# A streaming encoder layer on one core: the first adaLN columns shared between two engines, and second norm and token forms as one chain

## The chip, the core and the metric

The kernel runs on one core of a Trainium2 chip. The core has a matrix engine (TensorE, PE in the profile), two element-wise engines (VectorE, DVE; ScalarE, ACT), a general engine (GpSimd, POOL), and SyncE (SP), whose queue issues most transfers. Each works through its own list of instructions in order and waits at semaphores for the others. TensorE reads SBUF and writes PSUM, which is a set of banks that other engines must empty. The metric is the device time of one execution in microseconds, lower is better.

## The reference, cut to what matters

One layer over 1024 prompt frames and 32 sample frames, width 1024, in float32. The two groups of frames have a conditioning vector each, so that every adaLN column exists twice.

```python
mod = jax.nn.silu(c) @ w_ada + b_ada                       # (D,) @ (D, 6 D)
sh1, sc1, gt1, sh2, sc2, gt2 = jnp.split(mod[:, None, :], 6, axis=-1)
h = rmsnorm(x, g_mix) * (1 + sc1) + sh1
u = h @ w_in                                               # attention, mLSTM and gate columns
...                                                        # band attention, mLSTM
merged = (jax.nn.sigmoid(ga) * (ya @ w_br_att) + jax.nn.sigmoid(gm) * (ym @ w_br_mlstm))
x = x + gt1 * (merged @ w_out)
h2 = rmsnorm(x, g_ffn) * (1 + sc2) + sh2
g, up = jnp.split(h2 @ w_gate_up, 2, axis=-1)
x = x + gt2 * ((jax.nn.silu(g) * up) @ w_down)
```

Keys and values of the last 512 frames are outputs too. A final RMSNorm ends it.

## The kernel before, in words

All activations lie transposed, features on the 128 partitions in 8 row tiles of 1056 tokens (1024 + 32), which are cut into three column tiles of 352 (`TILES`). A float32 product is made of three fast ones (`PASSES`): each operand is split into a rounded part, which ScalarE writes, and the rest, which an element-wise engine subtracts. The helper `unit` computes one block of 128 output features on one column tile: 8 row tiles x 3 passes = 24 products into one PSUM bank (`mm`, three banks). `split_to` splits weights (L373 ScalarE, L374 VectorE or GpSimd).

The order on PE, ACT, DVE and POOL is the order in which the program is written; SP's order is a scheduler's. `Weights` loads and splits weight blocks ahead of their use: `advance` splits up to `ahead` blocks past the one in use and loads three raw blocks. `Side` runs generators beside the units: each unit gives 4 ticks, and a job takes `steps / ticks` steps a tick; `drain` runs what is left of it.

**Front.** While the inputs load, x is transposed (L300), its squares are summed, and `first_ada` multiplies silu(c) with the first 2048 columns of `w_ada`: for each of 8 row tiles k, 16 blocks of 128 columns on TensorE (L338), where the moving operand repeats the two conditions over 128 columns. Blocks 0 to 7 are the shift (bank psS), 8 to 15 the scale (psT). After the first k come the broadcast of the norm's factor (L263, L267), eight multiplications of x with it (L325) and the split of the first two weight blocks. `first_mod` adds the bias to the columns. `first_units` then runs the first two blocks of `w_in` (k and v of head pair 0) on all tiles at once, with `first_h` per row tile: VectorE scales and shifts (L362), ScalarE rounds (L363), VectorE subtracts (L364), and 18 products follow (L429). The third block (q) is an ordinary unit.

**Norm and FFN.** `second_norm(tiles)` is a side job: sums of squares by one-column products (L1478, L1479), a power on GpSimd (L1484), a `yield`, a broadcast through TensorE (L263), and then a step for each row tile: scale (L1495, VectorE), shift and round (L1496, ScalarE), low part (L1506, VectorE). It runs for the first column tile beside the last two column tiles of `w_out`, and for the other two beside the first FFN units. The first three FFN blocks are plain (`gate_unit`, `up_unit`, with the product on VectorE, L1643). Beside them `early_forms` makes sums and differences of the normed tokens (L1550, in turn on GpSimd and VectorE, L1560 and L1563 the split), four turns over row tiles. The later FFN blocks multiply these forms (`fifteen_products`, L1688), and `late_forms` makes the last of them. Before L1688 starts, the PSUM pools of the plain units are closed, so that their last evacuation must be done.

## Time and profile before

| | |
|---|---|
| median of 3 runs | 1672.52 us (1672.14 to 1672.92) |
| the profiled execution | 1671.17 us |
| its span, first to last instruction | 1669.2 us |
| mean granted TensorE clock | 0.99 |
| TensorE busy | 1605.7 us (96%) |
| VectorE, ScalarE, GpSimd busy | 67%, 47%, 32% |
| DMA | 192.47 MB, 115 GB/s on the mean |

In the rows, L and a number is a line of the kernel before. A timeline row is the start in us, the length, the engine, the line, the operation, output<-input, shapes, the count of merged instructions and, in brackets, the idle time before it and who ended it. A row of a line or tile has min/median/max of one instruction in ns, then first and last start. A matrix product is two rows of the profile for four-byte operands of the front (L338, L263, L1478), one for the rounded ones (L429, L407).

### The profile page before, as it was taken

The page shows a single profiled execution, that of the slowest core. Times are in us where ns is not written, and L with a number is a line of the kernel's source. Part 1 is how long each engine was busy: PE and PEld are TensorE (multiplying, and loading weights), DVE is VectorE, ACT ScalarE, POOL GpSimd, SP SyncE. Part 2 cuts the span into 40 slices and gives each one's busy share as a digit, 9 for nine tenths or more (in the row PEclk, how much of TensorE's full clock was granted, in tenths as well). Part 3 has the DMA queues.
Part 4 walks back from the last instruction along what each step waited for, and adds up shares of the span by engine and source line. Part 5 has one row for each costly group of instructions (what it writes and reads, how often), then busy time and mean ns, then how long its engine had stood idle before and what let it go on. Part 6 is the DMA issues. An engine that isn't in the chain of part 4 may idle for free.

```text
span 1669.2 us, 27636 instructions
## 1 busy us (share of the span) xinstructions
PE 1605.7 (96%) x10396; PEld 1580.4 (95%) x10396; DVE 1113.6 (67%) x2083; ACT 777.3 (47%) x1724; POOL 534.1 (32%) x540
## 2 busy tenths in 40 slices
PE   7989999999999999999999997999999999998997
PEld 6879999999999999999999997999999999998997
DVE  5446564646685755546655578989888886698754
ACT  3255454543455634444434444454544444444443
POOL 0043333423342311000012136556565652233101
PEclk9999999999999999999999899999999999999999
DMA  9533223332222332474453210222223136426453
GB/s 342 208 99 102 82 85 94 90 101 94 77 87 75 68 94 72 116 273 155 127 149 115 81 52 26 89 78 90 90 65 102 65 100 221 138 68 223 138 157 122
DMA packets 210328, 192.47 MB, mean 115 GB/s; under 512 B 10570, under 2 KB 180530, under 8 KB 209170
## 3 DMA queue, kind: packets, MB, share of 16 engines
q1 hardware_dynamic: 210194, 190.70, 36.3%
q8 instruction: 82, 1.34, 0.3%
q14 instruction: 52, 0.43, 0.1%
HBM read 152.19 MB, written 41.63 MB: 116 GB/s over the span
## 4 chain that ended last, share of the span: by engine, by line
PE 78%; DVE 8%; issue 3%; ACT 2%; POOL 1%; DMA 1%; DVEq 0%; POOLq 0%; ACTq 0%
PE mm L407 35%; PE psb L1688 23%; PE psb L2044 5%; PE mm L794 3%; PE psb L1929 3%; PE psV L694 2%; PE psS L636 1%; DVE wsp L374 1%; PE psT L663 1%; DVE s L1563 1%; DVE sl L1550 1%; DVE s L374 1%; POOL t L1253 1%; DMA wraw<-in_w_down_dram 1%; DVE s L1951 1%
## 5 line engine op out<-in xcount | busy, mean ns | idle before, releaser
L407 PE MATMUL mm<-s,wsp 128*128 128x352 f32 x4176 | 707.1, 325 | 10.4 <-DVE t L1643 4.5
L407 PEld LDWEIGHTS mm<-s,wsp 128*128 128x128 f32 x4176 | 671.6, 189 | 14.5 <-DVE t L1643 5.1
L1688 PE MATMUL psb<-s,wsp 128*128 128x352 f32 x2544 | 424.2, 324 | 16.2 <-DVE t L1643 6.1
L1688 PEld LDWEIGHTS psb<-s,wsp 128*128 128x128 f32 x2544 | 413.5, 190 | 18.9 <-issue 9.8
L374 DVE TENSOR_TENSOR wsp<-wraw,wsp 128x512 fp32r<-128x512 f32 (+1 forms) x284 | 246.4, 885 | 131.3 <-ACT wsp L373 129.7
L373 ACT ACTIVATE wsp<-wraw 128x512 fp32r<-128x512 f32 x342 | 202.4, 617 | 145.1 <-PE psb L1688 83.8
L656 POOL TENSOR_SCALAR st<-st,mx 128x640 f32<-128x640 f32 (+5 forms) x72 | 56.7, 787 | 192.7 <-DVE mx L655 178.4
L374 POOL TENSOR_TENSOR wsp<-wraw,wsp 128x512 fp32r<-128x512 f32 x58 | 76.6, 1342 | 108.3 <-ACT wsp L373 107.8
L1110 DVE SCALAR_TENSOR_TENSOR t<-wa,cmix,t 128x512 f32<-128x512 f32 x112 | 89.8, 807 | 8.6 <-DMA wa<-in_w_ada_dram 8.2
L2044 PE MATMUL psb<-s,wsp 128*128 128x352 f32 x528 | 86.9, 324 | 0.0
L2044 PEld LDWEIGHTS psb<-s,wsp 128*128 128x128 f32 x528 | 84.9, 188 | 0.0
L650 DVE CUSTOM_DVE_ANT_0 st<-psS,bias 128x640 f32<-128x640 f32 (+5 forms) x72 | 44.5, 618 | 57.0 <-PE psS L636 44.0
L1688 PE MATMUL psb<-x,wsp 128*128 128x352 f32 x432 | 79.3, 322 | 2.9 <-DVE x L1563 2.9
L651 ACT ACTIVATE st<-st,mx 128x640 f32<-128x640 f32 (+5 forms) x72 | 47.9, 665 | 68.9 <-DVE mx L650 68.8
L1525 POOL TENSOR_TENSOR t<-t,sl 128x352 f32<-128x352 f32 x18 | 17.6, 978 | 185.1 <-ACT sl L1523 185.1
L1688 PEld LDWEIGHTS psb<-x,wsp 128*128 128x128 f32 x432 | 71.0, 188 | 3.2 <-DVE x L1563 3.2
L670 ACT ACTIVATE pT<-psT 128x640 fp32r<-128x640 f32 (+3 forms) x80 | 38.6, 493 | 72.4 <-PE psT L663 57.3
L1726 DVE TENSOR_TENSOR t<-t,psb 128x352 f32<-128x352 f32 x120 | 60.4, 511 | 4.6 <-PE psb L1688 4.4
L1330 POOL TENSOR_TENSOR wraw<-wraw 128x512 f32<-128x512 f32 x25 | 37.0, 1480 | 78.3 <-DVE wsp L374 77.3
L675 DVE TENSOR_TENSOR pT<-psT,pT 128x640 fp32r<-128x640 f32 (+3 forms) x80 | 44.0, 558 | 20.6 <-ACT pT L670 20.4
L1330 POOL TENSOR_TENSOR wraw<-wraw,raw 128x512 f32<-128x512 f32 x33 | 55.8, 1703 | 0.9
L794 PE MATMUL mm<-s,s 128*128 128x264 f32 (+3 forms) x432 | 54.8, 283 | 0.0
(336 smaller groups left out, 2311.3 us busy)
## 6 DMA issues: line engine op xcount, KB each, us to landing
wraw<-in_w_in_dram SPq DMA_DIRECT2D x40, 512.0 KB
wraw<-in_w_gate_up_dram SPq DMA_DIRECT2D x33, 512.0 KB
wa<-in_w_ada_dram SPq DMA_DIRECT2D x64, 256.0 KB
wraw<-in_w_down_dram SPq DMA_DIRECT2D x32, 512.0 KB
a_d<-t SPq DMA_DIRECT2D x22, 528.0 KB
g_d<-t SPq DMA_DIRECT2D x16, 528.0 KB
x<-xres SPq DMA_DIRECT2D x16, 528.0 KB
t<-g_d SPq DMA_DIRECT2D x16, 528.0 KB
```

The lines of the kernel that those rows point to most:

```text
L373: act.activation(dst[:, 0], src, AF.Copy)
L374: eng.tensor_tensor(dst[:, 1], src, f(dst[:, 0]), op=ALU.subtract)
L407: pe.matmul(pt[:, :hi - lo], wt[(w0 + k) // 4][:, a, (w0 + k) % 4], xt[k][:, b, lo:hi], start=(k == 0 and q == 0), stop=(k == n - 1 and q ...
L651: act.activation(st[:n, :w], st[:n, :w], AF.Exp, bias=mx[:n, 1:2], scale=-1.0, accum_out=mx[:n, 2:3])
L656: pool.tensor_scalar(st[:n, :w], st[:n, :w], mx[:n, 3:4], 1.0, op0=ALU.mult, op1=ALU.mult)
L794: pe.matmul(pt[:n, :wd], hs[k][:, a, i * P:i * P + n], whl[b][:, k, :wd], start=(k == 0 and q == 0), stop=(k == KD - 1 and q == 2))
L1110: dve.scalar_tensor_tensor(ac[:, c], wa, cmix[:, c, k:k + 1], ac[:, c], op0=ALU.mult, op1=ALU.add)
L1330: pool.tensor_tensor(a(dst), a(x), a(y), op=op)
L1688: pe.matmul(acc, wt[:, a, k], x[k][:, b], start=(start and not onto and k == 0 and q == 0), stop=(stop and k == 3 and q == 2), skip_group_ ...
L1726: dve.tensor_tensor(c, c, y, op=ALU.add if sign > 0 else ALU.subtract)
L1929: pe.matmul(acc, wt[k // 4][:, u, k % 4], piece_of[k, i][:, v], start=(k == 0 and q == 0), stop=(k == KP - 1 and q == 2))
L2044: pe.matmul(acc, wt[(k - k0) // 4][:, u, (k - k0) % 4], piece_of[k, 2][:, v], start=(k == 0 and q == 0), stop=(k == NF - 1 and q == 2))
```

## The change

- *adaLN columns.* TensorE keeps blocks 6 to 15. For blocks 0 to 5 VectorE accumulates, for each condition, the row tiles of `w_ada` times silu(c) in SBUF (`acv`, 128 x 768, 16 passes), and 12 one-column products (6 blocks x 2 conditions) sum over the partitions. Two of the eight row tiles' loads and the weight loads change places in the program; the split of the first two weight blocks moves from k = 0 to k = 3, and a third raw block is asked for before `xres` is written.
- *First steps.* The eight multiplications L325 are gone: `scaled_x` multiplies x by scale and norm factor in one pass. The shift is ScalarE's bias in the rounding, and is added again in the low part. `scaled_x` of the next row tile is written before the low part of this one. The shift columns of the first two row tiles are computed first. In the first row tile the products with the rounded part come first; in the last they go by column tile.
- *Third block.* q's weights go into a slot instead of the small buffers, are split by GpSimd, and their split is written behind the seventh row tile of the first units.
- *Stores.* The eight key and value stores are issued by ScalarE instead of SP.
- *Second norm.* Five yields instead of one stand behind the power. The job for the first column tile is spread over 50 ticks.
- *Chain.* The norm of the later tiles and the early forms are one job, 9 steps in 10 ticks, not started by a step of its own; before a column tile's first unit it is run until that tile is normed. The pieces for the forms are numbered by turn, and their slots are taken when first needed. The bodies of `early_forms`, `late_forms`, `gate_unit` and `up_unit` move up in the file.

On VectorE, at the end of the adaLN columns and the start of the first units, before (s_348 and s_351 are x, s_506 and s_529 its split form, s_283 and sh_282 the scale and shift columns):

```order
L374 TENSOR_TENSOR wsp_369<-wraw_309,wsp_369 128x512
L352 TENSOR_TENSOR s_283<-psT_281,cols 128x16
L354 SCALAR_TENSOR_TENSOR s_283<-s_283,cols 128x16
L352 TENSOR_TENSOR sh_282<-psS_280,cols 128x16
L362 TENSOR_SCALAR s_348<-s_348,s_283,sh_282 128x1024
L362 TENSOR_SCALAR s_348<-s_348,s_283,sh_282 128x32
L364 TENSOR_TENSOR s_506<-s_348,s_506 128x1056
L362 TENSOR_SCALAR s_348<-s_348,s_283,sh_282 128x1024
L362 TENSOR_SCALAR s_348<-s_348,s_283,sh_282 128x32
L364 TENSOR_TENSOR s_529<-s_348,s_529 128x1056
```

And now (t_282 and t_283 are the accumulators, s_462 and s_508 the scaled x, s_479 and s_505 its split form; line numbers are the changed file's):

```order
L343 SCALAR_TENSOR_TENSOR t_283<-s_317,csil,t_283 128x768
L361 TENSOR_TENSOR s_285<-psT_281,cols 128x16
L364 SCALAR_TENSOR_TENSOR s_285<-s_285,cols 128x16
L373 SCALAR_TENSOR_TENSOR s_462<-s_123,s_285,t_279 128x1024
L373 SCALAR_TENSOR_TENSOR s_462<-s_123,s_285,t_279 128x32
L361 TENSOR_TENSOR sh_284<-psS_280,cols 128x2x2
L373 SCALAR_TENSOR_TENSOR s_462<-s_123,s_285,t_279 128x1024
L373 SCALAR_TENSOR_TENSOR s_462<-s_123,s_285,t_279 128x32
L384 SCALAR_TENSOR_TENSOR s_479<-s_462,sh_284,s_479 128x1024
L384 SCALAR_TENSOR_TENSOR s_479<-s_462,sh_284,s_479 128x32
L361 TENSOR_TENSOR sh_284<-psS_280,cols 128x2x6
L373 SCALAR_TENSOR_TENSOR s_508<-s_124,s_285,t_279 128x1024
```

The scaling of the next row tile now stands ahead of the low part of this one, and both are two-input passes on 1024 and 32 columns.

On ScalarE, at the end of the first units, before (wsp_706 and wsp_707 are q's weights, mm_503 to mm_505 k's banks):

```order
L363 ACTIVATE s_644<-s_357 128x1056
L363 ACTIVATE s_667<-s_357 128x1056
L466 ACTIVATE s_690<-mm_503 64x352 x2
L466 ACTIVATE s_690<-mm_504 64x352 x2
L469 ACTIVATE kf_691<-mm_504 128x192
L466 ACTIVATE s_690<-mm_505 64x352 x2
L469 ACTIVATE kf_691<-mm_505 128x352
L373 ACTIVATE wsp_706<-wraw_366 128x512
L373 ACTIVATE wsp_707<-wraw_366 128x512
```

And now (s_640 is q's weights):

```order
L380 ACTIVATE s_633<-s_610,sh_284 128x1024
L380 ACTIVATE s_633<-s_610,sh_284 128x32
L394 ACTIVATE s_640<-wraw_319 128x512 x2
L380 ACTIVATE s_665<-s_610,sh_284 128x1024
L380 ACTIVATE s_665<-s_610,sh_284 128x32
L497 ACTIVATE s_688<-mm_476 64x352 x2
```

q's split stands before the last row tile instead of behind k's evacuation.

On TensorE, at the second norm of the later tiles, before (psV holds the sums, rs the factors, mm_9883 is the first FFN unit's bank):

```order
L1478 MATMUL psV_9835<-ones,t_8935 96x1
L1479 MATMUL psV_9835<-ones,sl_9831 96x1
L407 MATMUL mm_9883<-s_9347,wsp_9768 128x352 x3
L407 MATMUL mm_9883<-s_9379,wsp_9768 128x352 x3
L407 MATMUL mm_9883<-s_9423,wsp_9768 128x352 x3
L407 MATMUL mm_9883<-s_9451,wsp_9768 128x352 x3
L263 MATMUL mm_9896<-ident,rs_9836 128x128 x2
```

And now (mm_9851 and mm_9900 are the first two units' banks):

```order
L428 MATMUL mm_9851<-s_9549,wsp_9759 128x352 x3
L1512 MATMUL psV_9864<-ones,t_8925 128x1
...
L1513 MATMUL psV_9864<-ones,sl_9822 96x1
L428 MATMUL mm_9851<-s_9577,wsp_9760 128x352 x3
L428 MATMUL mm_9851<-s_9621,wsp_9760 128x352 x3
...
L428 MATMUL mm_9900<-s_9577,wsp_9828 128x352 x3
L428 MATMUL mm_9900<-s_9621,wsp_9828 128x352 x3
L263 MATMUL mm_9919<-ident,rs_9865 128x128 x2
```

The sums stand behind the first 12 products, and 30 products instead of 12 stand between them and the broadcast.

The diff, cut to its core (bodies that only move are left out):

```diff
+    psA = [ps_s(), ps_t()]
+    NV = 6
+    acv = [tmpt((P, NV * P)) for _ in range(2)]
+
+    def first_ada():
+        load_ada(6)
+        W.load(2)
+        load_ada(KD)
+        W.load(3)
+        for k in range(KD):
+            c = csil[:, k].unsqueeze(1).to_broadcast([P, DH, 2])
+            for b in (*range(8, 16), *range(NV, 8)):
+                out = psA[b // 8][:, (b % 8) * P:(b % 8 + 1) * P]
+                pe.matmul(out.rearrange("p (r c) -> p r c", c=2), was[k][:, b * P:(b + 1) * P], c,
+                          start=(k == 0 and b in (NV, 8, 12)), stop=(k == KD - 1), skip_group_check=True)
+            for c in range(2):
+                if k == 0:
+                    dve.tensor_scalar(acv[c], was[k][:, :NV * P], csil[:, k, c:c + 1], None, op0=ALU.mult)
+                else:
+                    dve.scalar_tensor_tensor(acv[c], was[k][:, :NV * P], csil[:, k, c:c + 1], acv[c],
+                                             op0=ALU.mult, op1=ALU.add)
+            if k == 0:
+                bcast_cols(RB, rstd, [P] * 8 + [TS], 0)
+            if k == 3:
+                W.advance()
+        for b in range(NV):
+            for c in range(2):
+                pe.matmul(psA[0][:, b * P + c:b * P + c + 1], acv[c][:, b * P:(b + 1) * P], ones[:, 0:1],
+                          start=(b + c == 0), stop=True, skip_group_check=True)
...
-        dve.tensor_tensor(xns[j], xTs[j], RB, op=ALU.mult)
+        for c, a, b in col_segments(0, T):
+            dve.scalar_tensor_tensor(xns[j][:, a:b], xTs[j][:, a:b], s1[:, c, j:j + 1], RB[:, a:b],
+                                     op0=ALU.mult, op1=ALU.mult)
 
     def first_h(j):
+
         h = slot([P, 2, T], F32R)
         for c, a, b in col_segments(0, T):
-            x = xns[j][:, a:b]
-            dve.tensor_scalar(x, x, s1[:, c, j:j + 1], sh1[:, c, j:j + 1], op0=ALU.mult, op1=ALU.add)
-        act.activation(h[:, 0], xns[j], AF.Copy)
-        dve.tensor_tensor(h[:, 1], xns[j], f(h[:, 0]), op=ALU.subtract)
+            act.activation(h[:, 0, a:b], xns[j][:, a:b], AF.Identity, bias=sh1[:, c, j:j + 1])
+        if j + 1 < KD:
+            scaled_x(j + 1)
+        for c, a, b in col_segments(0, T):
+            dve.scalar_tensor_tensor(h[:, 1, a:b], xns[j][:, a:b], sh1[:, c, j:j + 1], f(h[:, 0, a:b]),
+                                     op0=ALU.add, op1=ALU.subtract)
...
-                split_to(t[:, :, :n], raw[:, 4 * i:4 * i + n], pool if W.done and not hm_n[1] else dve)
+                split_to(t[:, :, :n], raw[:, 4 * i:4 * i + n], pool if (W.done or home is slots) and not hm_n[1] else dve)
...
             first_h(k)
...
+            if k == 0:
+                first_mod(0, 2)
+                W.ahead = 3
+            if k == 6:
+                W.advance()
+
+            order = [(i, q, t) for i in range(2) for q in PASSES for t in range(3)]
+            if k == 0:
+                order.sort(key=lambda x: x[1][1])
+            if k == KD - 1:
+                order.sort(key=lambda x: (x[0], x[2]))
...
-        sp.dma_start(out[0, 0].rearrange("(i p) h d -> p i (h d)", p=P)[:, :, hp * P:(hp + 1) * P], stg)
+        act.dma_start(out[0, 0].rearrange("(i p) h d -> p i (h d)", p=P)[:, :, hp * P:(hp + 1) * P], stg)
...
-        w = w_cols(QA + hp * P)
+        w = w_cols(QA + hp * P, None if hp else slots)
...
-    first_mod()
+    first_mod(1)
+    scaled_x(0)
+    first_mod(0, 0, 2)
...
         pool.tensor_tensor(rs[:, 1], rs[:, 0], mhalf[:, :8], op=ALU.pow)
-        yield
+        for _ in range(5):
+            yield
         bcast_cols(rb2, rs[:, 1], [b - a for a, b in subs], a0)
...
+        normed[lo] = normed.get(lo, 0) + 1
...
-            while i >= len(room):
-                t = slot([P, 2, T], F32R)
-                room.extend(piece(t, n) for n in range(3))
+            while i >= len(room) or room[i] is None:
+                t, n = slot([P, 2, T], F32R), i - i % 3
+                room.extend([None] * (n + 3 - len(room)))
+                room[n:n + 3] = [piece(t, n) for n in range(3)]
...
-            job = side.start(second_norm(parts[0]), 11, 40)
+            job = side.start(second_norm(parts[0]), 15, 50)
...
-    job = side.start(second_norm(parts[1]), 19, 30)
-    side.step(job)
+    job = side.start(chain(second_norm(parts[1]), early_forms()), 9, 10)
     W.ahead = 4
     acts = [tmpt(), tmpt()]
     for t in TILES:
-        if t is TILES[2]:
-            side.drain(job)
-            job = side.start(early_forms(), 32, 30)
+        while normed.get(t[0], 0) < KD:
+            side.step(job)
```

113 lines of the change are left out of this document (51 added, 62 removed).

## The prediction

> **What bounds the kernel now.** I read first the page's busy times, then TensorE's waits, then its granted clock around these waits, then the timelines of the two places that the change touches.
>
> ```profile
> PE 1605.7 (96%) x10396; PEld 1580.4 (95%) x10396; DVE 1113.6 (67%) x2083; ACT 777.3 (47%) x1724; POOL 534.1 (32%) x540
> ```
>
> TensorE sets the end: 1605.7 of 1669.2 us. Outside its idle time and its half-speed time there is nothing to gain, and every us removed there moves all that follows. The view of waits names the up unit's product (L1643) for the largest wait behind the input loads:
>
> ```profile
> PE psb L1688 <- DVE t L1643: 6.1, 1, 6.1
> ```
>
> The windows (columns: stretch, length, then busy us of PE, PEld, DVE, ACT, POOL, then granted clock) show that such waits cost twice: the clock is then granted at about 0.50 for a while.
>
> ```profile
> 57.00:60.60 3.60, 3.60 (x14) 3.31 (x14) 2.40 (x4) 1.08 (x1) 0.00 (x0) 0.53 0.50 178
> ...
> 88.00:91.30 3.30, 3.30 (x13) 3.23 (x13) 0.00 (x0) 0.59 (x2) 3.24 (x4) 0.50 0.51 132
> 934.50:944.70 10.20, 7.33 (x29) 6.88 (x28) 5.29 (x10) 2.42 (x5) 4.63 (x1) 0.50 0.53 155
> 1019.80:1026.60 6.80, 4.85 (x17) 4.88 (x18) 3.93 (x10) 0.90 (x3) 4.78 (x3) 0.50 0.53 158
> ```
>
> TensorE was busy 3.6, 3.3, 7.3 and 4.9 us in these; half of each is lost.
>
> **The front, start of the first units.** TensorE's timeline of before:
>
> ```profile
> 22.78 2.05 PE L338 MATMUL psT<-csil,s 128*128 128x128 f32 x16
> 24.67 1.95 PE L338 MATMUL psS<-csil,s 128*128 128x128 f32 x16
> 26.46 2.28 PE L263 MATMUL mm<-ident,rstd 128*128 128x128 f32 x18
> ...
> 52.00 1.95 PE L338 MATMUL psS<-csil,s 128*128 128x128 f32 x16
> 56.39 2.54 PE L429 MATMUL mm<-s,wsp 128*128 128x352 f32 x9 [2.44 <-ACT s L363]
> ```
>
> Eight column blocks are 16 rows and 1.79 us (24.67 to 26.46), 0.224 us a block; 16 blocks for each of 8 row tiles fill 22.78 to 53.95 with the broadcast between. Six blocks of each tile leave, so TensorE has 2.24 us a tile: from 22.78, with 2.2 us of broadcast, it is through at 42.9 if it never waits. VectorE gets 16 passes over 768 columns. The rows for their price, for the weight splits that stand between tile 3 and tile 4, and for the transfers:
>
> ```profile
> L1110 DVE SCALAR_TENSOR_TENSOR t<-wa,cmix,t x112: 718/742/1822, 118.1 to 712.1; 128x512 f32<-128x512 f32 x112
> ```
>
> ```profile
> 34.36 1.15 ACT L373 ACTIVATE wsp<-wraw 128x512 fp32r<-128x512 f32 x2 [0.50 <-DMA wraw<-in_w_in_dram]
> ```
>
> ```profile
> 38.52 2.49 DVE L374 TENSOR_TENSOR wsp<-wraw,wsp 128x512 fp32r<-128x512 f32 x4
> ```
>
> ```profile
> 35.00:40.00 5.00, 5.00 (x47) 5.00 (x46) 5.00 (x7) 0.51 (x1) 0.00 (x0) 1.00 0.99 406
> ```
>
> The same accumulate takes 0.742 us on 512 columns; at about 1.04 ns an element 768 columns are 1.0, issued some 0.95 apart. Tiles 0 to 3 end before the splits, whose last ScalarE half ends at 35.5; four splits at 0.62 run behind it and end near 36.2. Tiles 4 to 7 are then 8 x 0.95 = 7.6: VectorE ends at 43.8. The last row tile lands behind three transfers of 1024 KB after the second weight block of 34.36: at 406 GB/s 2.6 us each, 42.1, then two passes, 44.0. So 44.0, and TensorE's own blocks of that tile end at 44.4. Next are 12 one-column products, 24 rows; by the one-column rows quoted below (24 rows in 2.58 us) 2.6, so 47.0. First shift columns 0.2, ScalarE's part of the first tile, Identity with a bias on 1024 columns, some 1.15 (before it took 1.08 for a Copy of 1056, the row here), and semaphores: the first product of the first units at **48.5** instead of 56.39.
>
> ```profile
> 55.25 1.08 ACT L363 ACTIVATE s<-s 128x1056 fp32r<-128x1056 f32 x1 [19.74 <-DVE s L362]
> ```
>
> Bounds: 47.0 if the one-column products run faster, 51.0 if VectorE's passes take 1.3.
>
> **Pace of the first units.** VectorE's rows of before:
>
> ```profile
> 54.20 1.02 DVE L362 TENSOR_SCALAR s<-s,s,sh 128x1024 f32<-128x1024 f32 x2
> 56.37 1.26 DVE L364 TENSOR_TENSOR s<-s,s 128x1056 fp32r<-128x1056 f32 x1 [1.15 <-ACT s L363]
> 57.54 1.02 DVE L362 TENSOR_SCALAR s<-s,s,sh 128x1024 f32<-128x1024 f32 x2
> ```
>
> Each row tile is a closed loop VectorE, ScalarE, VectorE of 3.4 us (54.20, 57.54), while 18 products need 2.9 us at full clock (9 in 1.45). In the change ScalarE reads what VectorE scaled one tile earlier, and VectorE issues the next scaling before the low part, so the loop opens: VectorE has two passes of 1024+32 columns a tile, by the price above 1.4 each, 2.8 us, just under TensorE's 2.9. Before took 27.3 us (56.39 to 83.67, where the 2.36 of row 86.03 begin); now 8 x 2.9, plus 1.7 for a half-clock window as at 57.0, plus 0.5 for v's first bank, which the change's second write of shift columns releases only after the first low part: 25.4. End at 73.9, **9.8 us earlier**. Bounds: 23.2 (no clock loss) to 27.3 (VectorE the bound).
>
> [...]
>
> **The third block (q).** Its split is moved from behind the first units into them, in a slot, on GpSimd.
>
> ```profile
> 86.03 0.43 PE L407 MATMUL mm<-s,wsp 128*128 128x352 f32 x1 [2.36 <-ACT wsp L373]
> 87.38 4.02 PE L407 MATMUL mm<-s,wsp 128*128 128x352 f32 x14 [0.92 <-POOL wsp L374]
> ```
>
> 2.36 + 0.92, and 1.7 of half clock at 88.0: **5.0 us**. Cover: the split starts when ScalarE is past tile 6 and takes 2 x 1.3 on GpSimd, some 5 us ahead of its use. What is late next is the bank of k's first tile; with the last row tile's products ordered by tile it is free 2.4 us before the units end.
>
> **Stores on ScalarE's queue.**
>
> ```profile
> L494 SPq DMA_DIRECT2D out_dram<-stg x8: 388/394/534, 92.6 to 313.7; - x8
> ```
>
> Eight issues of 0.4 move from SP, where other loads queue, to ScalarE, where the next unit's evacuation stands behind them. ScalarE is 47% busy; I take a quarter as showing, **-0.8 us** (0 to -3.2).
>
> **Second norm and forms.** TensorE before:
>
> ```profile
> 930.78 0.28 PE L1478 MATMUL psV<-ones,t 128*128 128x1 f32 x2
> ...
> 933.36 2.96 PE L407 MATMUL mm<-s,wsp 128*128 128x352 f32 x12
> 939.19 2.87 PE L263 MATMUL mm<-ident,rs 128*128 128x128 f32 x12 [2.87 <-POOL rs L1484]
> 941.77 7.33 PE L407 MATMUL mm<-s,wsp 128*128 128x352 f32 x36
> 948.94 7.84 PE L407 MATMUL mm<-s,s 128*128 128x352 f32 x48
> 956.62 7.84 PE L407 MATMUL mm<-s,wsp 128*128 128x352 f32 x48
> ```
>
> A pair of units is 7.68 us (948.94 to 956.62), a tick 0.96. Now the sums come 12 products into the first unit, 30 products stand between them and the broadcast, 4.8 us, and the splits of fb 1's weights stand ahead of the power on VectorE:
>
> ```profile
> L1484 POOL TENSOR_TENSOR rs<-rs,mhalf x2: 1649/3343/5037, 872.6 to 934.1; 128x8 f32<-128x8 f32 x2
> ```
>
> 5.04 is the power beside VectorE's splits, 1.65 alone; it now runs alone. So the 2.87 goes, and at least half of the 10.2 us at half clock. But TensorE being early does not shorten the end if VectorE is late. VectorE's ledger, from the windows of before:
>
> ```profile
> 972.60:1016.80 44.20, 38.58 (x238) 37.72 (x236) 39.98 (x56) 18.38 (x42) 25.39 (x24) 1.00 0.15 49
> 941.90:968.20 26.30, 26.30 (x158) 26.30 (x158) 19.94 (x51) 21.09 (x51) 0.00 (x0) 0.95 0.02 5
> ```
>
> ```profile
> 1015.23 1.26 DVE L1550 TENSOR_TENSOR x<-x 128x352 f32<-128x352 f32 x1
> 1016.41 0.51 DVE L1563 TENSOR_TENSOR s<-sl,s 128x352 fp32r<-128x352 f32 x1
> 1016.85 0.51 DVE L1643 TENSOR_TENSOR t<-mm,sl 128x352 f32<-128x352 f32 x1
> ...
> 1021.10 0.51 DVE L1643 TENSOR_TENSOR t<-mm,sl 128x352 f32<-128x352 f32 x1
> ```
>
> The norm is 19.9 us of VectorE in 26.3, the four turns of forms 44.2 with their waits for GpSimd (39.98 busy), the tail from 1016.85 to L1688's start at 1021.75 4.9. Before, the forms could not start until the third tile's units, 972.6. As one chain they follow the norm at once: 942.0 + 19.9 + 44.2 + 4.9 = 1011.0, with up to 1.7 more if a half-clock window delays the broadcast; I take 1012.2, **9.5 us earlier**. TensorE alone would end its first pair at 930.78 + 2.58 + 2.3 + 7.68 = 943.3 and the ninth at 943.3 + 8 x 7.68 = 1004.7, so about 7 us of waits on L1643 stay. Bounds: 2 (only the first stall pays) to 12.
>
> The five empty steps and the spread of the first norm cost nothing: before shows no TensorE wait there. The moved function bodies and the other numbering of pieces change no instruction.
>
> **Sum.** Start and pace 9.8, q 5.0, stores -0.8, norm and forms 9.5: 23.5 us. The profiled execution took 1671.17 (span 1669.2 and 1.97 around it): 1647.7. The median shown is 1.35 above it: **1649**.
>
> [...]
>
> **Rivals.**
> (a) The forms keep their end. For it: VectorE's 44.2 us is a chain with GpSimd, and denser neighbours (the norm's ScalarE work, the sl buffers) could stretch it; against: it starts 10 us earlier. Then only a little of 9.5 is left: 14 us, 1658.5.
> (b) The first units become VectorE's. 2.8 against 2.9 is a thin margin: at 3.4 a tile, and a start at 50, front and q give 9, in all 17.5: 1655.
> (c) Slower: ScalarE blocked by its stores. Each store waits on the semaphore of a transfer eight issues earlier, such as a weight load that SP itself holds back, and every evacuation stands behind it. It decides from 24.3 / 8 = 3 us a store; at 4 us the kernel is 1680. Against: those transfers are issued a whole block earlier.
> (d) The change doesn't do what it says: the transfers, not the engines, pace the front, and the first units wait for the adaLN rows as before. Against: 34.36 and 406 GB/s put the last row tile 8 us ahead of its old use (52.00 less 1.8). No change: 1672.
>
> **How the numbers follow.** Forecast 0.66, (a) 0.14, (b) 0.13, (c) 0.04, (d) 0.03. The forecast's bounds taken together (the low ends 8.7 for front and q, 2, -3.2; the high ends 18, 12, 0) would be 7.5 to 30; 8 in 10 lie between 1641 and 1662, which takes in (a) and (b). This kernel's runs tell 0.2% from no change: faster 0.93, same 0.03, slower 0.04.
>
> **What would show it.** In the changed profile: the first product of the first units near 48.5, these units over near 74, no wait of TensorE before the q block; no wait for rs; second norm's first pass at 942 less 14; forms starting about 20 us behind it, and one wait on the up product at L1688's start of 4 to 7 us. Wrong would be: VectorE rows above 1.3 us for 768 columns, gaps in the first units at the low part, TensorE waiting on ScalarE behind a store, or a turn of forms longer than 10.2 us.

## The result, and the profile after

The changed kernel takes 1645.88 us (median of four, 1642.54 to 1648.59) against 1672.72 us before (1672.14 to 1674.35): a ratio of 0.9837, 95% interval 0.9817 to 0.9857, or 26.8 us. Its profiled execution took 1642.54 us (span 1640.6), the fastest of the four. A sum made from two traces therefore gives 28.6 us, 1.8 more than the medians do.

In the rows of the changed kernel the line numbers are its own: L428 is the old L407, L460 the old L429, L1657 the old L1643, L1563 and L1576 the old L1550 and L1563 (forms), L1726 the old L1688, L787 the old L756.

The page's busy times of the changed kernel, then its view of waits (engine, tile and line <- who ended the wait: us in total, times, longest):

```profile
PE 1589.7 (97%) x10324; PEld 1566.7 (95%) x10324; DVE 1121.0 (68%) x2100; ACT 780.8 (48%) x1732; POOL 535.7 (33%) x540
```

```profile
PE psb L1726 <- DVE s L1989: 5.5, 4, 2.7
PE psb L1726 <- DVE wsp L395: 3.1, 3, 1.8
PE psb L1726 <- DVE x L1576: 2.3, 1, 2.3
PE mm L787 <- DMA t<-in_state_conv_dram: 2.2, 1, 2.2
PE psb L1726 <- DVE t L1657: 2.0, 1, 2.0
PE mm L428 <- DVE t L1657: 1.9, 1, 1.9
PE mm L428 <- ACT sl L1651: 1.7, 1, 1.7
```

The waits for the power (2.9), for q's split (2.4 and 0.9) and the long one for the up product (6.1) are gone. TensorE is busy 16 us less: 8 on adaLN columns (48 blocks of 0.224 less 2.74 for the one-column products) and 7.4 at half speed (in the half-clock stretches, granted 0.50, it was busy 22.5 us before and is 7.7 now, half of each lost; the stretch at the very end, which holds no product, is left out). The rest, some 0.6, is open. The front waits for the first rounded tile (1.4 instead of 2.4), and one wait has grown: L787, for the load of the convolution state, from 0.8 to 2.2. The last three rows, 5.6 together, are what is left ahead of the forms' first product of the 10.6 that TensorE waited there for up products (4.5 and 6.1); the trace puts the 1.7 among them down to ScalarE.

Where the time went is read by comparing the start of the same product in both traces. TensorE's timeline of the changed kernel:

```profile
48.43 1.44 PE L460 MATMUL mm<-s,wsp 128*128 128x352 f32 x6 [1.44 <-ACT s L380]
...
73.65 2.64 PE L428 MATMUL mm<-s,s 128*128 128x352 f32 x15
76.13 0.60 PE L511 MATMUL mm<-ident,kf 128*128 128x128 f32 x4
...
374.28 0.24 PE L787 MATMUL mm<-ident,t 24*128 24x24 f32 x1 [2.18 <-DMA t<-in_state_conv_dram]
...
972.80 4.10 PE L428 MATMUL mm<-s,wsp 128*128 128x352 f32 x24 [1.69 <-ACT sl L1651]
978.82 1.39 PE L428 MATMUL mm<-s,wsp 128*128 128x352 f32 x7 [1.92 <-DVE t L1657]
...
996.56 3.76 PE L1726 MATMUL psb<-s,wsp 128*128 128x352 f32 x22 [2.03 <-DVE t L1657]
```

And two rows of the kernel before that the prediction did not need, the first transpose of k (behind the first pieces of q) and the transpose of the convolution state:

```profile
91.20 0.68 PE L480 MATMUL mm<-ident,kf 128*128 128x128 f32 x4
...
388.08 0.24 PE L756 MATMUL mm<-ident,t 24*128 24x24 f32 x1 [0.82 <-DMA t<-in_state_conv_dram]
```

| Place | before | now | gain up to there | predicted |
|---|---|---|---|---|
| first product of the first units | 56.39 | 48.43 | 8.0 | 7.9 |
| end of the first units | 83.67 | 73.65 | 10.0 | 9.8 |
| first transpose of k, behind q's first products | 91.20 | 76.13 | 15.1 | 14.8 |
| transpose of the convolution state | 388.08 | 374.28 | 13.8 | 14.0 |
| first product with the forms | 1021.75 | 996.56 | 25.2 | 23.5 |
| whole span | 1669.2 | 1640.6 | 28.6 | 23.5 |

The windows of the changed kernel (stretch, length, busy us of PE, PEld, DVE, ACT, POOL, granted clock):

```profile
49.30:52.70 3.40, 3.14 (x12) 2.71 (x11) 3.40 (x8) 1.91 (x4) 0.00 (x0) 0.50 1.03 415
...
922.00:932.00 10.00, 10.00 (x68) 10.00 (x68) 5.14 (x17) 5.46 (x10) 1.65 (x1) 1.00 0.54 147
996.60:1003.40 6.80, 6.80 (x43) 6.80 (x44) 5.08 (x9) 3.10 (x8) 6.04 (x3) 1.00 0.52 157
1015.30:1022.10 6.80, 4.47 (x16) 4.02 (x15) 6.17 (x10) 1.74 (x5) 3.04 (x2) 0.50 0.19 55
```

Half speed stays at the start of the first units, is gone around the norm's broadcast and behind the forms' first product, and has come up new at 1015.3, where before there was none. So the gain behind 996.56 (2.9 us up to TensorE's last product) comes from no step that was aimed at it: with half of TensorE's busy time in a window as its cost, the windows before cost 2.4 at 1019.8 and 1.7 at 1456.7, the new one costs 2.2, and the waits for the splits and the late form are 1.4 shorter together (3.9 and 2.9 before, 3.1 and 2.3 now). That makes 3.3, close to the 2.9.

VectorE of the changed kernel, at the last adaLN tile, in the first units and along the chain; the GpSimd row is q's split:

```profile
41.97 1.95 DVE L343 SCALAR_TENSOR_TENSOR t<-s,csil,t 128x768 f32<-128x768 f32 x2 [0.31 <-DMA s<-in_w_ada_dram]
...
51.26 1.44 DVE L384 SCALAR_TENSOR_TENSOR s<-s,sh,s 128x1024 fp32r<-128x1024 f32 x2
...
53.98 1.44 DVE L384 SCALAR_TENSOR_TENSOR s<-s,sh,s 128x1024 fp32r<-128x1024 f32 x2
...
63.49 2.50 DVE L373 SCALAR_TENSOR_TENSOR s<-s,s,t 128x1024 f32<-128x1024 f32 x2
65.92 3.87 DVE L384 SCALAR_TENSOR_TENSOR s<-s,sh,s 128x1024 fp32r<-128x1024 f32 x4
...
64.10 4.28 POOL L395 TENSOR_TENSOR s<-wraw,s 128x512 fp32r<-128x512 f32 x2 [40.12 <-ACT s L394]
...
927.84 0.58 DVE L1530 SCALAR_TENSOR_TENSOR x<-x,amod,t 128x352 f32<-128x352 f32 x1 [4.53 <-ACT t L267]
...
948.07 0.52 DVE L1563 TENSOR_TENSOR sl<-x 128x352 f32<-128x352 f32 x1
...
990.03 1.26 DVE L1563 TENSOR_TENSOR x<-x 128x352 f32<-128x352 f32 x1
```

The last pair of accumulates ends at 43.9, a row tile of the first units takes VectorE 2.72 us (51.26 to 53.98), and the norm's first pass, the forms' first sum and their last sum start at 927.8, 948.1 and 990.0. The last pair waits 0.3 for the last row tile of `w_ada` to land, at 41.9, and TensorE waits as long for it: the front now starts as early as that transfer lets it.

### The profile page after: what moved, and what is told of

Same layout as the page of the kernel before. It is cut to its first block, busy times and chain, and to the rows that moved or that the text cites. A ratio compares the mean times of both kernels' runs of the same rounds, so it can differ in the third digit from the quotient of the medians.

```text
span 1640.6 us, 27517 instructions
## 1 busy us (share of the span) xinstructions
PE 1589.7 (97%) x10324; PEld 1566.7 (95%) x10324; DVE 1121.0 (68%) x2100; ACT 780.8 (48%) x1732; POOL 535.7 (33%) x540
## 4 chain that ended last, share of the span: by engine, by line
PE 79%; DVE 8%; ACT 3%; issue 2%; DMA 1%; POOL 1%; DVEq 0%; POOLq 0%; ACTq 0%
PE mm L428 35%; PE psb L1726 24%; PE psb L2082 5%; PE mm L825 3%; PE psb L1967 3%; PE psV L725 2%; PE psS L667 1%; DVE wsp L395 1%; PE psT L694 1%; DVE s L395 1%; DVE s L1576 1%; DVE s L1989 1%; DVE sl L1563 1%; DVE st L681 1%; PE psV L1059 1%
## 5 line engine op out<-in xcount | busy, mean ns | idle before, releaser
L428 PE MATMUL mm<-s,wsp 128*128 128x352 f32 x4104 | 690.4, 324 | 5.8 <-DVE t L1657 1.9
L428 PEld LDWEIGHTS mm<-s,wsp 128*128 128x128 f32 x4104 | 656.8, 188 | 9.0 <-DVE stg L518 2.3
L1726 PE MATMUL psb<-s,wsp 128*128 128x352 f32 x2544 | 422.0, 323 | 11.4 <-DVE s L1989 5.5
L1726 PEld LDWEIGHTS psb<-s,wsp 128*128 128x128 f32 x2544 | 410.9, 189 | 14.4 <-issue 6.1
L1726 PE MATMUL psb<-x,wsp 128*128 128x352 f32 x432 | 80.2, 325 | 2.3 <-DVE x L1576 2.3
L1726 PEld LDWEIGHTS psb<-x,wsp 128*128 128x128 f32 x432 | 71.5, 189 | 2.8 <-DVE x L1576 2.8
```

The costliest lines, as they stand in the source:

```text
L428: pe.matmul(pt[:, :hi - lo], wt[(w0 + k) // 4][:, a, (w0 + k) % 4], xt[k][:, b, lo:hi], start=(k == 0 and q == 0), stop=(k == n - 1 and q ...
L1726: pe.matmul(acc, wt[:, a, k], x[k][:, b], start=(start and not onto and k == 0 and q == 0), stop=(stop and k == 3 and q == 2), skip_group_ ...
```

## The experiments

All gains are of a median over the median of the kernel before that ran beside it. The changed kernel's is 26.8 us.

| | median us | gain us | ratio, 95% interval |
|---|---|---|---|
| front alone | 1660.89 | 12.1 | 0.9912 to 0.9941 |
| norm and forms alone | 1660.17 | 12.9 | 0.9907 to 0.9937 |
| all columns on TensorE | 1652.05 | 21.0 | 0.9858 to 0.9891 |
| q's split late | 1650.15 | 22.9 | 0.9848 to 0.9878 |
| stores on SyncE | 1649.79 | 22.9 | 0.9849 to 0.9876 |
| state of the convolution apart | 1643.41 | 30.2 | 0.9804 to 0.9833 |
| forms as a later job | 1651.38 | 22.3 | 0.9854 to 0.9889 |
| one empty step | 1649.88 | 23.8 | 0.9843 to 0.9876 |
| sums on VectorE | 1639.60 | 34.0 | 0.9776 to 0.9812 |
| sums on VectorE, state apart | 1637.38 | 35.3 | 0.9773 to 0.9800 |
| the same, weight sums on VectorE | 1643.02 | 29.6 | 0.9806 to 0.9833 |
| sums on VectorE, state apart, products spread | 1636.48 | 35.9 | 0.9770 to 0.9797 |

The changed kernel's own interval is 0.9817 to 0.9857, and some of these touch it. But of the five kernels that lost 3 to 6 us (all columns on TensorE, q's split late, stores on SyncE, forms as a later job, one empty step) no execution is as fast as the changed kernel's slowest, 1648.59, and of the three that are fastest (all with sums on VectorE, weight sums left on GpSimd) none is as slow as its fastest, 1642.54. A single trace also holds half-clock windows that other executions of the same kernel need not have, as the granted clocks in the last section show (0.989 to 0.995 for the changed kernel's four).

### The two halves apart

The front alone. Against the changed kernel, norm and forms go back to what they were:

```diff
-        for _ in range(5):
-            yield
+        yield
...
-    job = side.start(chain(second_norm(parts[1]), early_forms()), 9, 10)
+    job = side.start(second_norm(parts[1]), 19, 30)
+    side.step(job)
...
-        while normed.get(t[0], 0) < KD:
-            side.step(job)
+        if t is TILES[2]:
+            side.drain(job)
+            job = side.start(early_forms(), 32, 30)
```

> The kernel before with the front of the change alone (shared columns, overlapped first steps, q's split in a slot, stores on ScalarE's queue); second norm and forms as before. Theory: the two halves are independent. The first product starts at 48.4, the first units end at 73.7, no wait before q, so the front gives 15 us, some 1 to 2 of it lost again at the load of the convolution state; from there on all of the old waits return (rs 2.9, L1643 4.5 and 6.1, half clock at the norm), L1688's first product at 1021.75 less 13.8 = 1008, and the time at 1672.7 - 13.8 = 1659, 1657 to 1661. Rival: the halves need each other (SyncE's queue or the weights ahead shift), and the front alone gives under 11: above 1662.

Measured: 1660.89 us, 12.1 us gained, a little less than the 13.8 that was expected, within its range. TensorE's timeline has the old wait before the forms' first product (L1722 here):

```profile
1012.48 7.71 PE L1722 MATMUL psb<-s,wsp 128*128 128x352 f32 x34 [6.10 <-DVE t L1677]
```

That is 9.3 earlier than before instead of 13.8: in this execution the wait for the convolution state was 2.8 and half clock (0.50) followed for 6.8 us from 375.3, which neither the kernel before nor the changed one has in its trace. This profiled execution was the slowest of the four, 1661.94 us.

Norm and forms alone. Against the kernel before, whose front stays:

```diff
-        yield
+        for _ in range(5):
+            yield
...
-    job = side.start(second_norm(parts[1]), 19, 30)
-    side.step(job)
+    job = side.start(chain(second_norm(parts[1]), early_forms()), 9, 10)
```

> The kernel before with the chain of second norm and forms alone (five empty steps, norm and forms as one job); the front as before. Theory: independent halves. The first product of the first units at 56.4 as before, the last unit before the norm at the old time, L1688's first product 11.4 us earlier, at 1010.4, and the time 11 to 14 us under before: 1658.5 to 1661.5. Rival: the chain only paid because the front moved the work (other half-clock windows): under 8 us, above 1664.5.

Measured: 1660.17 us by the median, 12.9 us gained, as expected. The wait before the forms' first product is the changed kernel's, but the product comes at 1014.3, 7.5 earlier than before, where 1010.4 was expected:

```profile
1014.29 5.96 PE L1692 MATMUL psb<-s,wsp 128*128 128x352 f32 x26 [2.03 <-DVE t L1623]
```

The profiled execution was again the slowest of its four (1661.89). Of the missing 3.9, 2.1 were lost ahead of the first product (58.52 instead of 56.39; TensorE's last adaLN blocks are as late, 54.12 instead of 52.00) and 1.7 in a half-clock window of 3.4 us behind the norm's one-column products, at 937.2, which the changed kernel does not have.

12.1 and 12.9 make 25.0, the change gave 26.8: the halves are independent within what the medians tell.

### The parts of the front

All 16 column blocks on TensorE:

```diff
-    NV = 6
-    acv = [tmpt((P, NV * P)) for _ in range(2)]
+    NV = 0
...
-                          start=(k == 0 and b in (NV, 8, 12)), stop=(k == KD - 1), skip_group_check=True)
+                          start=(k == 0 and b % 4 == 0), stop=(k == KD - 1), skip_group_check=True)
-            for c in range(2):
+            for c in range(2 if NV else 0):
```

> The changed kernel with all 16 adaLN blocks on TensorE again (no accumulators on VectorE, no one-column products); first steps, q and the rest as changed. Theory: the share is what starts the first units early. TensorE needs 16 x 0.224 = 3.58 us a row tile from 23.2, with 2.2 of broadcast it ends at 54.0; the scale columns are ready 1.8 before that, so that only the shift columns and ScalarE's part stand behind it: first product at 55.6 instead of 48.4, all later work 7.2 us later, time +7. Rival: the transfers pace the front (the last row tile lands at 41.9 in the changed kernel): first product within 2 us of 48.4.

Measured: 5.8 us of the gain lost. TensorE works without a wait until its last block, and the first units follow it:

```profile
54.34 1.95 PE L336 MATMUL psS<-csil,s 128*128 128x128 f32 x16
57.73 1.24 PE L459 MATMUL mm<-s,wsp 128*128 128x352 f32 x6 [1.44 <-ACT s L379]
```

57.7 instead of 55.6, because this execution was 2.0 us later than the changed kernel already at the start of the blocks (25.1 instead of 23.2); the blocks then take what was worked out. It is 8.7 us behind the changed kernel at the first transpose of k and 7.5 from the convolution state on, where it waits 0.9 instead of 2.2; 2.0 of both is that delay. The transfers do not pace this front; the share does what the prediction charged it with.

q's weights in the small buffers again, split behind the first units:

```diff
-                W.ahead = 3
-            if k == 6:
-                W.advance()
...
-        w = w_cols(QA + hp * P, None if hp else slots)
+        w = w_cols(QA + hp * P)
...
-pool if (W.done or home is slots) and not hm_n[1] else dve
+pool if W.done and not hm_n[1] else dve
```

> The changed kernel with the third block's weights back in the small buffers, split behind the first units. Theory by the prediction's term: the waits of 2.4 and 0.9 us before q and one half-clock window come back, 5.0 us later from q on and 5.0 us on the time. Rival: no window follows, 3.3 us. Second rival: the front is now early enough that the split hides, within 1 us.

Measured: 3.9 us of the gain lost by the medians. In the trace the old waits are back:

```profile
76.40 0.42 PE L428 MATMUL mm<-s,wsp 128*128 128x352 f32 x1 [2.05 <-ACT wsp L394]
77.75 4.00 PE L428 MATMUL mm<-s,wsp 128*128 128x352 f32 x14 [0.93 <-POOL wsp L395]
```

Clock 0.50 follows for 3.4 us from 77.6. The first transpose of k starts at 81.58, 5.4 later than in the changed kernel, of which 0.7 was there at the end of the first units; 4.8 is the term, 5.0 was predicted.

The eight stores on SyncE's queue again:

```diff
-        act.dma_start(out[0, 0].rearrange("(i p) h d -> p i (h d)", p=P)[:, :, hp * P:(hp + 1) * P], stg)
+        sp.dma_start(out[0, 0].rearrange("(i p) h d -> p i (h d)", p=P)[:, :, hp * P:(hp + 1) * P], stg)
```

> The changed kernel with the eight key and value stores back on SyncE's queue. The prediction's term: the stores cost 0.8 us on ScalarE's queue (0 to 3.2), so this is 0.8 faster. Rival: they cost nothing, because no wait of TensorE in the changed kernel ends on a store: the same within 0.5 us in the trace at 375 us. Second rival: on SyncE's queue they hold loads back, slower by 1 to 3 us.

Measured: 3.9 us slower than the changed kernel, so the prediction's term had the wrong sign. Timelines of SyncE, ScalarE and TensorE in this kernel:

```profile
80.71 0.39 SPq L525 DMA_DIRECT2D out_dram<-stg  x1
...
85.06 0.60 ACT L524 ACTIVATE stg<-mm 128x512 f32<-128x512 f32 x1 [2.90 <-DMA out_dram<-stg]
...
85.71 5.67 PE L428 MATMUL mm<-s,s 128*128 128x352 f32 x24 [2.64 <-ACT stg L524]
```

and the first store of the changed kernel:

```profile
77.62 0.43 ACTq L525 DMA_DIRECT2D out_dram<-stg  x1
```

ScalarE issues the store right behind the copy that fills it, SyncE 3.1 us later, behind a weight load and two loads of the cache. So the two staging buffers come free late, ScalarE waits 2.9 for the next one, TensorE 2.64 for its bank (0.49 in the changed kernel, and 0.50 before), and 3.4 us at clock 0.50 follow (from 86.6). In the kernel before, the same loads were just in time, as its rows of ScalarE (the copy) and SyncE (the last cache load, the store) show:

```profile
91.91 0.60 ACT L493 ACTIVATE stg<-mm 128x512 f32<-128x512 f32 x1 [3.32 <-PE mm L480]
...
92.12 0.43 SPq L579 DMA_DIRECT2D t<-in_cache_v_dram  x1
...
92.65 0.39 SPq L494 DMA_DIRECT2D out_dram<-stg  x1
```

The copy ended at 92.51, the loads at 92.55. With the front 15 us earlier the copy comes first. A busy ScalarE did not hurt the changed kernel: ScalarE stood four times some 0.5 us behind an issue, but no wait of TensorE ends on a store.

### The wait that grew

The convolution state in a buffer of its own:

```diff
-        scr = tmpt((24, P))
+        scr = gp.tile([24, P], F32, name="scr")
```

> The changed kernel with the convolution state in a small buffer of its own; in the changed kernel its load waits for the store of an attention output from the same buffer (store issued at 368.75, load at 372.62, TensorE waits 2.18). Theory: the wait goes and all that follows is 2.2 us earlier. Rival: another load or a bank is late next and 1 us or less is left.

SyncE's queue in the changed kernel, a store of attention output and the load that takes over its buffer:

```profile
368.75 0.33 SPq L752 DMA_DIRECT2D ya_d<-t  x1
372.62 0.32 SPq L785 DMA_DIRECT2D t<-in_state_conv_dram  x1
```

and TensorE with the state apart, where the load was issued at 86.2:

```profile
371.48 0.24 PE L787 MATMUL mm<-ident,scr 24*128 24x24 f32 x1
```

No wait is left, the transpose starts 2.8 earlier, and the median is 2.5 us lower (30.2 us gained instead of 26.8, though the intervals of the two ratios overlap). So the 1.3 us that the change lost here came from a load that stands behind a store in flight (SyncE's own waits in the changed kernel have 3.5 us of L785 for the store `ya_d<-t`): TensorE arrived 15.1 us earlier, the load was issued only 14.0 earlier (386.61 before).

### What sets the forms' first product

Norm and forms as two jobs, the forms from the third column tile on:

```diff
-    job = side.start(chain(second_norm(parts[1]), early_forms()), 9, 10)
+    job = side.start(second_norm(parts[1]), 9, 10)
...
+        if t is TILES[2]:
+            side.drain(job)
+            job = side.start(early_forms(), 32, 30)
```

> The changed kernel with norm and forms as two jobs again: the norm at the changed pace with its five empty steps, the forms from the third column tile's first unit on. Theory: VectorE's chain sets L1688's start, so it moves with the forms' first sum: these start at about 951.5 instead of 948.1, and L1688 at 1000 instead of 996.6. Rival: what paid is TensorE's removed stall alone, and the chain nothing: L1688 within 1 us of 996.6.

Measured: 4.5 us of the gain lost. VectorE, then TensorE:

```profile
954.45 0.52 DVE L1563 TENSOR_TENSOR sl<-x 128x352 f32<-128x352 f32 x1
...
1003.59 6.64 PE L1729 MATMUL psb<-s,wsp 128*128 128x352 f32 x29 [6.11 <-DVE t L1657]
```

The forms start 6.4 us later (954.45 against 948.07; 951.5 was expected, but ahead of them VectorE waits 3.8 us for the second tile's last product), and the forms' first product comes 7.0 later. Of both, 2.0 have nothing to do with the edit: in this execution the wait for the convolution state was 3.1 instead of 2.2, and the norm's broadcast was already 2.0 late (928.19 against 926.15). That leaves 4.4 and 5.0. The forms' first product moves with the forms' first sum, as VectorE's ledger has it, and the single wait of 6.1 of the kernel before is back. The rival, that the chain itself paid nothing, is out.

One empty step behind the power instead of five:

```diff
-        for _ in range(5):
-            yield
+        yield
         bcast_cols(rb2, rs[:, 1], [b - a for a, b in subs], a0)
```

> The changed kernel with one empty step behind the power on GpSimd instead of five. TensorE then waits about 2.4 us for the power before the broadcast and runs at half clock behind it, 7 us together, while VectorE's first pass can start 1 us sooner. Theory (VectorE's chain sets L1688's start): L1688 within 2 us of 996.6, with the waits for L1657 smaller instead. Rival (TensorE's stall is what the change removed): L1688 5 to 8 us later, 1002 to 1004.

Measured: 3.0 us of the gain lost (the median is 4.0 above the changed kernel's), and here the rival was right. TensorE, VectorE, VectorE, TensorE:

```profile
925.16 2.88 PE L263 MATMUL mm<-ident,rs 128*128 128x128 f32 x12 [2.63 <-POOL rs L1518]
...
991.58 1.26 DVE L1562 TENSOR_TENSOR x<-x 128x352 f32<-128x352 f32 x1
...
998.98 1.29 DVE L395 TENSOR_TENSOR wsp<-wraw,wsp 128x512 fp32r<-128x512 f32 x2 [3.91 <-ACT wsp L394]
...
1002.60 7.60 PE L1725 MATMUL psb<-s,wsp 128*128 128x352 f32 x46 [0.88 <-DVE t L1656]
```

The wait for the power costs 2.6, and the half-clock window of 6.8 us behind it another 2.3 (half of 4.7 busy). One more window, at 984.5, costs 1.7, while the waits ahead of the forms are 1.1 shorter (0.6, 2.8, 0.2 and 0.9 instead of 5.6). That makes 5.5; the forms' first product is 6.0 later. VectorE's last early sum is only 1.5 later (991.58), and then VectorE idles 3.9 us for ScalarE's rounding of the weights, which stands behind the silu of a gate product, for which ScalarE itself had idled 6.2 us until TensorE was done with it (997.97). So VectorE's chain does not set the end alone.

TensorE waited 5.6 us in the changed kernel between the norm and the forms, more than the 5.0 that the power and its window cost, and yet these waits did not take the stall up. Why they shrank by 1.1 only is not shown. My reading is that with the chain four ticks further ahead in VectorE's list the up products still stood behind form sums.

### Sums on VectorE

All sums of the forms on VectorE instead of every other one on GpSimd:

```diff
-            return ((pool, dve)[turns[0] % 2], o, x, op, y)
+            return (dve, o, x, op, y)
```

> The changed kernel with all sums of the forms on VectorE (before, every other one on GpSimd). Theory: a VectorE row beside GpSimd takes 1.25 us instead of 0.51, and VectorE waits 1.1 to 1.2 us a turn for a sum of GpSimd; alone, 12 sums and 6 low parts of 0.44 make 7.9 us a turn instead of 10.15, TensorE's steps pace it at 8.5, the waits for L1657 (3.9 and 1.7 behind ScalarE) go, and L1688 starts near 991 instead of 996.6. Rival: VectorE is full of its own work, the 24 sums add 24 x 0.44 = 10.6 us to it: L1688 at 1007.

Measured: 1639.60, 7.2 us more gained than by the change (6.3 between the two medians). The windows over the four turns of forms, in the changed kernel and in this one:

```profile
948.10:991.20 43.10, 39.49 (x245) 38.82 (x244) 37.09 (x56) 17.10 (x41) 26.04 (x24) 1.00 0.15 51
```

```profile
949.30:987.50 38.20, 38.20 (x240) 38.20 (x239) 37.21 (x82) 17.22 (x40) 0.00 (x0) 1.00 0.17 57
```

VectorE is busy for the same 37 us, with 82 instructions instead of 56: the 26 us of GpSimd cost VectorE as much in longer rows as doing the work itself, and its 6 us of waiting, 4.5 of them for sums of GpSimd, go on top. TensorE runs through (38.20 of 38.20), and the forms' first product is at 992.5 instead of 996.6 (991 was expected; this execution was 1.2 late at the norm's broadcast), with 0.9 of wait left.

Sums on VectorE and the state apart, in one kernel (the two diffs above):

> The changed kernel with all sums of the forms on VectorE and the convolution state in a buffer of its own. Theory: the two gains (6.3 and 2.5 us on the medians) lie in places far apart and add: 1645.9 - 8.8 = 1637, 1634 to 1640. Rival: they are mostly half-clock windows that come and go, and together give under 5: above 1641.

Measured: 1637.38 us (1635.04 to 1639.36), 8.5 below the changed kernel's where the theory had 8.8: the gains add.

On top of that, the weight sums of the first group of forms on VectorE as well:

```diff
-                    pool.tensor_tensor(a(dst), a(x), a(y), op=op)
+                    self.eng.tensor_tensor(a(dst), a(x), a(y), op=op)
...
-    fifteen = [Fifteen(hk_rows[i:i + 3]) for i in range(0, len(hk_rows), 3)]
+    fifteen = [Fifteen(hk_rows[i:i + 3], dve if i == 0 else pool) for i in range(0, len(hk_rows), 3)]
```

> The same kernel, and the weight sums of the first group of forms (L1361, ten of 1.5 us on GpSimd) on VectorE too. Theory: beside them VectorE's rows of 0.5 and 0.7 us take 1.2 to 2.0, 6.7 us too much between 997 and 1016, so TensorE's waits of 1.8 for the split weights and 1.8 for a late form and the half clock behind them (5.1) go: 4 to 7 us faster than with the sums on GpSimd. Rival: ten sums of 0.62 on VectorE cost as much as they free, and the waits stay: the same within 1 us.

Measured: 5.6 us slower than without it (1643.02); both theories missed. VectorE's groups from 989 to 1016 (instructions, busy us, mean ns of one, idle before), with the weight sums on GpSimd and then on VectorE:

```profile
L395 DVE TENSOR_TENSOR wsp<-wraw,wsp 128x512 fp32r<-128x512 f32 x9 | 9.0, 1013 | 1.2 <-ACT wsp L394 1.2
```

```profile
L395 DVE TENSOR_TENSOR wsp<-wraw,wsp 128x512 fp32r<-128x512 f32 x8 | 5.4, 690 | 4.5 <-ACT wsp L394 4.5
...
L1361 DVE TENSOR_TENSOR wraw<-wraw,wraw 128x512 f32<-128x512 f32 x4 | 2.7, 684 | 0.0
```

The rows do get short (690 ns instead of 1013), but VectorE now waits 4.5 us for ScalarE's rounding of the weights. A weight sum, its rounding and its low part follow on each other; on one engine's list the second half stands behind ScalarE and holds up all that comes after. The forms' sums did not have this, because each is split one or two steps later. That this is the whole loss is my reading of the rows; a half-clock window that is longer here (6.8 instead of 3.4 us, at 1011.5) is part of it, and no run takes the two apart.

### One-column products and the clock

With sums on VectorE and the state apart, the norm's sums of squares in three groups between products:

```diff
             pe.matmul(pt[:b - a, i:i + 1], sq[:, a - lo:b - lo], ones[:, 0:1], start=False, stop=True)
+            if i in (1, 3) and len(subs) > 4:
+                yield
...
-        for _ in range(5):
+        for _ in range(3 if len(subs) > 4 else 5):
             yield
```

> The kernel with the forms' sums on VectorE and the convolution state apart, and the second norm's one-column products (24 rows in 2.4 us, no wait of TensorE among them) in three groups of eight between the first units' products; three empty steps behind the power instead of five, so that the broadcast stays in its place. Theory: a dense stretch of one-column products is what brings the half-clock window of 3.4 us at 918.5, as waits do elsewhere; spread, it goes, and all that follows is 1.7 us earlier (median 1635.7). Rival: the window does not come from these products, or the spread sums make the power late for the broadcast (0.5 us of margin): no gain, or 1 to 3 us slower.

The window right behind these products (916.3 to 918.9 in one piece), then the same stretch with them spread:

```profile
918.50:921.90 3.40, 3.40 (x14) 3.40 (x14) 2.14 (x10) 0.51 (x1) 1.07 (x1) 0.50 0.78 225
```

```profile
918.50:921.90 3.40, 3.40 (x29) 3.40 (x29) 2.74 (x11) 2.23 (x4) 0.00 (x0) 1.00 0.59 172
```

The half-clock window is gone, without TensorE having waited in either. Where such windows fall differs from one trace to the next (937.2 with norm and forms alone, 918.5 here), but the spread products no longer stand that close together: any 3.4 us of that stretch hold at most some 1.5 us of them, against 2.0 in the window before this one, and the last section has what followed such amounts in the traces. The median is 1636.48, 0.9 lower, which these runs do not tell from no change; in the changed kernel's trace the window was not there to begin with. It is the fastest version of the study: a ratio of 0.9784 (0.9770 to 0.9797) to the kernel before, where the change gave 0.9837 (0.9817 to 0.9857).

## Why the prediction was right, and where it was off

**Front, start: right.** VectorE's last accumulate at 44.0 (measured 43.9), the one-column products through at 47.0 (44.26 + 2.74), the first product at 48.5 (48.43). The price of about 1.04 ns an element, added to a row of another shape (0.742 us on 512 columns), held: 1.01 us for one pass of 768 columns, 1.95 for two. That the share carries it is shown: without it 5.8 us are lost. The last row tile, put at 42.1, landed at 41.9 and was waited for, so that transfer bounds the start as well now.

**Pace: right.** 25.4 was worked out, 25.2 measured. VectorE takes 2.72 a tile, not 3.4, so rival (b) is out, and half speed at the start came as summed (clock 0.50 from 49.3 to 52.7).

Beside GpSimd's split of q (4.28 us from 64.10) VectorE took longer: its rows at 63.49 and 65.92 take 2.50 and 3.87 us where 1.44 and 2.88 are usual, 2.05 us in all. TensorE did not wait for it, since VectorE was that far ahead.

**Third block: right.** 5.0 predicted, 4.8 measured by putting it back.

**Stores: wrong.** The step that failed is the one that says ScalarE's evacuations stand behind the issues and 0.8 us show. They did stand behind them, but no wait of TensorE came of it, and leaving the stores on SyncE would have cost 3.9. What I did not ask is what the old place costs once the front is faster: SyncE then issues the first store 3.2 us after its data is there, and the staging buffers are two. The rows for it stood in the trace of before: SyncE's loads ended at 92.55, the copy at 92.51.

**Not seen: the convolution state, 1.3 us.** The load stands behind a store from the same buffer, and the wait of 0.8 before the change was a warning that I left out.

**Norm and forms: right in mechanism, 1.9 us too small.** First pass at 942.0 less 14 (927.84), the norm 20.2 us (19.9 summed), forms and tail 48.5 (49.1). The 1.2 that I added for half speed at the broadcast did not come; the clock is 1.00 from 922 to 932. The wait that stays was forecast as one of 4 to 7 at the forms' first product; it is 2.0 there, and 5.6 in three pieces of about 2 when the two ahead of it are counted. That VectorE alone sets the end is too simple, as the run with one empty step shows: a stall of TensorE came out in full at the forms' first product, though VectorE's last early sum was only 1.5 later.

**Behind the forms: 2.9 us that no step of mine has**, from half-clock windows that fell elsewhere and from shorter waits. The sum of 28.6 therefore owes 2.9 to nothing that was forecast. Together with 0.5 us at the very end: 10.0 + 5.1 - 1.3 + 11.4 + 2.9 + 0.5 = 28.6 for this execution. The median lies 3.3 above it, and so 3.1 below the forecast of 1649.

**The other rivals.** (a) is out: the forms' end moved by 11.4, and a turn of forms kept its length (43.1 us for the four, 44.2 before). (c) is out with the stores. (d) is out: with all columns on TensorE the time went up.

## What to carry to other kernels

When a stage gets faster, look through the trace for everything that was just in time for the old pace (a store that frees a buffer, a load behind that store): loads that ended just as a copy did and a wait of 0.8 us were worth 3.9 and 2.5 us here. Work given to GpSimd beside a busy VectorE saved nothing, because VectorE rows of 0.51 us took up to 1.27 beside it; taking it back was worth 6 to 7 us for the forms' sums, and lost 5.6 for the weight sums, whose next step waits for ScalarE. Two engines that handed results back and forth within a few us of each other had no single bound here: a stall put back on TensorE came out again in full at the forms' first product, although TensorE was waiting 5.6 us for the other side.

## What the runs showed of the hardware

The changed kernel's four executions spread over 6 us, and the mean granted clock goes with it: 0.995, 0.994, 0.993 and 0.989 at 1642.5, 1645.0, 1646.7 and 1648.6 us. Where half speed fell can be counted in the traces. In the kernel before, the half-clock stretches (0.50) start at 57.22, 87.94, 934.45, 1019.78, 1456.68 and 1661.48 us: 9, 257, 282, 410 and 470 times 3.413 us behind the first. In the changed kernel they start at 49.28, 1015.25 and 1633.07, 283 and 464 times 3.413 behind the first. So it is in each of the traces: the starts lie on a grid of 3.41 us that is fixed for that execution. But for the last, which the end of the kernel breaks off, the stretches are 3.41, 3.41, 10.24, 6.83 and 3.41 us long before and 3.41 and 6.83 now, one to three steps of the grid. I divided the TensorE time of 14 traces (both kernels and all experiments, 60 to 1625 us) into windows by this grid, left out those that already run at half speed, and summed in each the time without a product of more than one column:

| Such time in a window | windows | followed by half speed |
|---|---|---|
| 1.85 us or more | 37 | 37 |
| 1.70 to 1.85 us | 16 | 6 |
| 0.5 to 1.70 us | 239 | 0 |

These are counts of this case and no more; why the clock went down is not shown. One wait lay in a single window, another in two. In the kernel before, 2.15 us of such time lie in the one window from 1453.27, and a half-clock stretch follows in which TensorE is busy 3.4 us, so that 1.7 are lost. In the changed kernel the wait of 2.18 for the convolution state falls into two, 1.45 us in the window to 373.55 and the rest behind it, and the clock stays at 1.00.

Dense one-column products stood ahead of half speed as waits did. In the kernel before, the window from 931.03 has 2.29 us of them and 0.04 of idle time, and half speed follows at 934.45. With sums on VectorE and the state apart, 2.0 us of them fell into one window and half speed followed, while in the changed kernel the grid parts them at 919.68 into 0.65 and 1.57 and it did not. The front's half-clock window, which the prediction kept in its sum, follows a window with both: 1.13 us of one-column products and 1.44 of waiting, from 45.87 to 49.28.
